# A two-layer hybrid mixer kernel: another order and other instructions in the attention loop

## Chip, core and metric

The kernel runs on one core of a Trainium2 chip. The metric is device time in microseconds (us), the median of three runs. The engines are named as in the profile: PE is TensorE (PEld its weight loads), DVE VectorE, ACT ScalarE, POOL GpSimd, SP the engine that issues most DMAs.

## What is computed

Two layers run over 1024 latent tokens and 256 context tokens of width 1024. Each layer normalises and modulates its input, multiplies it with one wide input matrix, feeds four mixers (attention, pooling, a state space, a gated MLP), gates their outputs and multiplies with an output matrix. The change touches the attention alone:

```python
q = (_rms(cq, g_q) @ w_uq).reshape(b, n, MLA_HEADS, MLA_NOPE + MLA_ROPE)      # 4 heads, 64 + 32
s = einsum('bqhd,bkhd->bhqk', qn, k_nope) + einsum('bqhr,bkr->bhqk', qr, k_rope)
p = softmax(s * 96 ** -0.5)                   # maximum over the keys taken off first
o = einsum('bhqk,bkhd->bqhd', p, v)           # then times the SiLU gate
```

Latent queries see 1280 keys, context queries (first layer only) the 256 context keys. All in float32.

## The kernel before, in words

Scores are kept transposed: keys on the partitions, queries on the columns. One step of the loop (`w`, line 1477) is one head `h` of a pair of heads `v` on 256 queries. Its 1280 keys make five PSUM banks of two key tiles each (`BANKS`, line 1212), each bank 128 x 512. Layer 1 has 8 pairs, 16 steps; layer 0 has the same and two short pairs for the context queries, with one bank a step.

The order on PE, DVE, ACT and POOL is written out by hand (line 1476): each engine runs its instructions as the Python calls come. One step does this:

- `scores(v, h, 1..4)`: 24 products of 256 columns fill banks 1 to 4 (three products for each key tile: high and low parts). ACT copies bank 0 into `acc` (line 1338), DVE takes the maximum of `acc` and each further bank, column halves apart (line 1340), and folds the two halves (line 1342).
- `vals(.., 0)`: probabilities times values of the pair before, in float32. `PVS` (line 37) says how many of the step's five key tiles go into each of three slots. The two heads write the two halves of the output's partitions.
- `maxima`: PE transposes `acc` (line 1354), DVE reduces over what are now columns (line 1356), negates and splits the result in a high and a low part (`m4`, lines 1358 and 1359).
- `vals(.., 1)`; then `rows`: PE turns `m4` into four rows (line 1365) and DVE spreads them into `row` (line 1367).
- `scores` of bank 0 of the next head (line 1502), into the sixth buffer of the ring of score banks (five `mm` and one `tp`).
- in even steps `finish`: sums of the probabilities of the pair before by a product with ones (line 1431), and their reciprocals over 128 x 256 (line 1435). In odd steps the two products with the gate (lines 1437 and 1438).
- `shift` (line 1369): for each bank a product of four rows with ones adds minus the maximum to the scores (line 1376); then ACT takes the exponentials (line 1389), which frees the bank, and POOL adds them up.

Transposed maxima, sums and one score bank in six share a pool of two PSUM banks (`tp`): a tile taken from it waits until the one before in its bank has been read. In every even step the query projection of the next pair stands between scores and values (`q_pair`), and in some odd steps that of the next 256 queries (`q_chunk`), with DVE's part of `q_pair` (line 1300) ahead of `rows`.

Of the kernel before, what the change touches and what calls it, by code (L numbers as in the profile page):

```python
# [12 lines left out]
F32 = mybir.dt.float32  # L13
# [23 lines left out]
PVS = (((0, 2), (2, 5), (5, 5)), ((0, 2), (2, 5), (5, 5)), ((0, 2), (2, 5), (5, 5)), ((0, 3), (3, 5), (5, 5)))  # L37
# [38 lines left out]
def tile_hybrid_backbone(ctx: ExitStack, tc: tile.TileContext, A):  # L76
# [23 lines left out]
    stg = [""]  # L100
# [64 lines left out]
    rmask = const.tile([4, 2], F32, name="rmask")  # L165
    add(V, rmask, ident[0:4, 0:2], ident[0:4, 2:4])
    ones4 = const.tile([4, 128], F32R, name="ones4")
    V.tensor_copy(ones4, ones[0:4, :].to_broadcast([4, 128]))
# [1045 lines left out]
    def attention(l, last, blocks, out):  # L1214
# [99 lines left out]
        def scores(v, h, banks):  # L1314
# [8 lines left out]
            for i, kts in list(enumerate(BANKS if c0 < NLAT else BANKS[0:1]))[banks.start:banks.stop]:  # L1323
# [11 lines left out]
                for x in range(2):  # L1335
                    a, p = acc[:, n * x:n * x + n], ps[:, n * x:n * x + n]
                    if i == 0:
                        d["first"] = lambda: S.copy(acc, d["b"][0])
                    else:
                        tt(V, a, a, p, ALU.max)  # L1340
# [8 lines left out]
        def maxima(v, h):  # L1349
            d = st[v, h]  # L1350
            stg[0] = "mx"
            d["tp"] = tp = tp_ps()
            for j in range(2):
                T.transpose(tp[:, 128 * j:128 * j + 128], d["acc"][:, 128 * j:128 * j + 128], ident)
            m = sml.tile([128, 2], F32, tag="mx", name="mx")
            V.tensor_reduce(out=m, in_=tp[:, 0:n].rearrange("p (j k) -> p j k", j=2), axis=AX.X, op=ALU.max)
            d["m4"] = m4 = sml.tile([128, 4], F32, tag="m4", name="m4")
            ts(V, m4[:, 0:2].bitcast(F32R), m, -1.0, ALU.mult)
            stt(m4[:, 2:4], m, -1.0, m4[:, 0:2], ALU.mult, ALU.subtract)

        def rows(v, h):

            d = st[v, h]
            tp = d["tp"][0:4, 256:384]
            T.transpose(tp, d["m4"], ident)
            d["row"] = row = sml.tile([4, 2, 128], F32R, tag="row", name="row", bufs=2)
            mul(V, row, tp.unsqueeze(1).to_broadcast([4, 2, 128]), rmask.unsqueeze(2).to_broadcast([4, 2, 128]))

        def shift(v, h):

            c0, pr = pairs[v]
            d = st[v, h]
            stg[0] = "sh"
            rv = d["row"].rearrange("p j q -> p (j q)").unsqueeze(1).to_broadcast([4, 2, n])
            for ps in d["b"]:
                T.matmul(ps, lhsT=ones4, rhs=rv, start=False, stop=True, skip_group_check=True)  # L1376
# [44 lines left out]
        def finish(v):  # L1421
# [8 lines left out]
            for h in range(2):  # L1430
                T.matmul(tp[64 * h:64 * h + 64, 0:n], lhsT=ones.to_broadcast([128, 64]), rhs=st[v, h]["sm"][:, 0:n],
                         start=True, stop=True, skip_group_check=True)
            yield "fdve"
            rs = qp[0].tile([128, n], F32, tag="rs", name="rs", bufs=2) if v < nv - 1 else s2("rs")[:, 0:n]
            V.reciprocal(out=rs, in_=tp[:, 0:n])
            yield "av"
            mul(V, gs, st[v][:, 0:n], gs)
            mul(V, gs, rs, gs)
# [37 lines left out]
        with tc.manual_schedule(engines={mybir.EngineType[x] for x in MAN}):  # L1476
            for w in range(2 * nv):
# [16 lines left out]
                k = [range(5 * h + i, 5 * h + j) for i, j in PVS[w % 4]]  # L1494
# [6 lines left out]
                if w + 1 < 2 * nv:  # L1501
                    scores((w + 1) // 2, 1 - h, range(0, 1))
                vals(v, w, k, 2)
                if h and short:
                    go("fend")
                    go("fdve")
                if h:
                    go("av")
                if not short:
                    go("fend")  # L1510
                    go("fdve")
# [7 lines left out]
                shift(v, h)  # L1519
                if w == 2 * fresh[-1] - 3:  # L1520
                    out.scales()
# [19 lines left out]
            go("fdve")  # L1541
# [509 lines left out]
```

## Time and profile before

| | |
|---|---|
| median of three runs | 1442.95 us (1437.25 to 1455.37) |
| profiled execution | 1443.26 us, span 1441.5 us |
| granted TensorE clock, mean | 0.94 |
| busy share | PE 88%, PEld 69%, DVE 65%, POOL 38%, ACT 32% |
| chain that ended last | PE 51%, DVE 28%, issue 7%, POOL 6%, DMA 3%, ACT 3% |
| attention loops | 481 to 672 us (layer 0), 1177 to 1343 us (layer 1) |

The span is divided by engine; an engine that is off the chain of waits may idle for nothing. The two loops hold 357 us of the 1441.5 us. Within them one step takes 9 to 10 us, and the question in each is which wait ends last before `shift` can run.

### The profile page before, as it was taken

To read this page: it belongs to the slowest core of one execution; us is meant where nothing else is said; L and a number is where in the kernel's file an instruction comes from. 1 tells how busy PE (TensorE), PEld (TensorE's weight loads), DVE (VectorE), ACT (ScalarE), POOL (GpSimd) and SP (SyncE) were. 2 spreads that over 40 slices of the span, in tenths; PEclk is the share of its full clock that TensorE was granted. 3 is DMA by queue.
4 is the path that set the end of the run, shared out by engine and by line. 5 is a ranking of instruction groups with operands and counts; after the bars stand their busy time and mean duration, and the time that the engine had idled before them with its cause. 6 is when DMAs were issued, how large, how long until landed. Compare 5 with 4: busy or idle time off the path is not lost.

```text
span 1441.5 us, 20269 instructions
## 1 busy us (share of the span) xinstructions
PE 1271.1 (88%) x7558; PEld 992.0 (69%) x7558; DVE 937.8 (65%) x1974; ACT 464.8 (32%) x879; POOL 552.8 (38%) x580
## 2 busy tenths in 40 slices
PE   4877986999999998999999769987699999999997
PEld 1555764779888766766777657765488787766785
DVE  8685399623552576757799882699426447767566
ACT  2341220120343644445233422301213454544300
POOL 2476241301002345655444591314001126656343
PEclk9988997999998999999999979998799999999999
DMA  9435321665321100014122454412752020000421
GB/s 314 143 103 179 122 86 46 152 178 132 89 53 33 27 22 1 1 45 131 45 82 95 107 155 147 122 44 59 149 146 65 8 59 23 15 16 16 146 103 73
DMA packets 124679, 127.33 MB, mean 88 GB/s; under 512 B 40908, under 2 KB 98724, under 8 KB 124582
## 3 DMA queue, kind: packets, MB, share of 16 engines
q1 hardware_dynamic: 118886, 111.86, 26.3%
q0 software_dynamic: 2880, 9.54, 2.8%
q10 hardware_dynamic: 2816, 4.65, 0.9%
q8 instruction: 59, 0.97, 0.3%
q14 instruction: 38, 0.31, 0.1%
HBM read 97.47 MB, written 25.94 MB: 86 GB/s over the span
## 4 chain that ended last, share of the span: by engine, by line
PE 51%; DVE 28%; issue 7%; POOL 6%; DMA 3%; ACT 3%; SPq 1%; POOLq 0%; ACTq 0%; DVEq 0%
PE mm_sc L1330 7%; PE mm_out L1632 6%; PE mm_in L154 5%; PE mm_in L152 5%; DVE H L131 5%; PE mm_in L153 5%; PE av L1411 3%; DVE stmp L131 3%; DVE z L148 3%; PE mm_sc L1376 2%; DVE op L131 2%; DVE acc L131 2%; POOL op L131 1%; DVE xres L145 1%; PE tp_sc L1330 1%
## 5 line engine op out<-in xcount | busy, mean ns | idle before, releaser
L154 PE MATMUL mm_in<-hT,wlo 128*128 128x512 f32 (+1 forms) x696 | 264.6, 381 | 26.9 <-DVE wlo L131 26.9
L152 PE MATMUL mm_in<-hT,whi 128*128 128x512 f32 (+1 forms) x696 | 270.4, 390 | 0.4 <-ACT whi L635 0.4
L153 PE MATMUL mm_in<-hT,whi 128*128 128x512 f32 (+1 forms) x696 | 264.8, 381 | 5.8 <-POOL hT L131 3.1
L154 PEld LDWEIGHTS mm_in<-hT,wlo 128*128 128x128 f32 x696 | 137.6, 198 | 53.3 <-DVE wlo L131 29.4
L152 PEld LDWEIGHTS mm_in<-hT,whi 128*128 128x128 f32 x696 | 137.8, 199 | 35.8 <-issue 14.2
L1632 PE MATMUL mm_out<-wo,yh 128*128 128x512 f32 x576 | 161.4, 394 | 0.5 <-POOL wo L131 0.4
L153 PEld LDWEIGHTS mm_in<-hT,whi 128*128 128x128 f32 x696 | 138.2, 199 | 31.1 <-POOL hT L131 5.7
L1632 PEld LDWEIGHTS mm_out<-wo,yh 128*128 128x128 f32 x576 | 107.5, 189 | 25.5 <-issue 1.0
L635 ACT CAST whi<-wraw 128x1024 fp32r<-128x1024 f32 x38 | 42.6, 1122 | 192.4 <-PE mm_in L153 142.8
L131 DVE TENSOR_TENSOR acc<-acc,mm_sc 128x256 f32<-128x256 f32 x216 | 77.4, 417 | 39.9 <-PE mm_sc L1330 36.8
L131 DVE TENSOR_TENSOR wlo<-wraw,whi 128x1024 fp32r<-128x1024 f32 x38 | 58.0, 1532 | 67.1 <-ACT whi L635 61.0
L131 POOL TENSOR_TENSOR psum<-pE 128x512 f32<-128x512 f32 (+1 forms) x36 | 47.1, 1308 | 135.8 <-ACT pE L1389 135.8
L1632 PE MATMUL mm_out<-wo,yl 128*128 128x512 f32 x288 | 92.0, 392 | 0.6 <-POOL yl L131 0.6
L131 POOL TENSOR_TENSOR psum<-psum,pL 128x512 f32<-128x512 f32 x64 | 83.1, 1298 | 5.0
L131 DVE TENSOR_TENSOR H<-H,stmp 128x80 f32<-128x80 f32 x248 | 75.2, 362 | 0.8
L131 DVE TENSOR_TENSOR stmp<-a,H 128x160 f32<-128x160 f32 x124 | 54.8, 476 | 14.5 <-POOL pws L131 7.2
L144 POOL TENSOR_SCALAR srs<-smv 128x1 f32<-128x1 f32 x18 | 5.6, 312 | 152.6 <-DVE smv L1062 152.6
L1389 ACT ACTIVATE pE<-mm_sc 128x512 f32<-128x512 f32 x55 | 30.6, 594 | 102.3 <-PE mm_sc L1376 102.3
L1632 PEld LDWEIGHTS mm_out<-wo,yl 128*128 128x128 f32 x288 | 54.3, 189 | 12.5 <-POOL yl L131 1.0
L144 POOL TENSOR_SCALAR rs_z<-mv_z 128x1 f32<-128x1 f32 x18 | 18.5, 1029 | 114.7 <-DVE mv_z L1664 114.7
L1783 ACT ACTIVATE G<-mm_in 128x512 f32<-128x512 f32 (+1 forms) x40 | 22.2, 554 | 115.9 <-PE mm_in L154 115.9
L1330 PE MATMUL mm_sc<-QA,KT 96*128 96x256 f32 x372 | 56.8, 305 | 0.0
(360 smaller groups left out, 2805.8 us busy)
## 6 DMA issues: line engine op xcount, KB each, us to landing
wmod<-in_w_mod_dram SPq DMA_DIRECT2D x48, 512.0 KB, 4.5
wraw<-in_w_in_dram SPq DMA_DIRECT2D x36, 512.0 KB, 4.4
wor<-in_w_out_dram SPq DMA_DIRECT2D x16, 512.0 KB, 3.6
s5u<-Sd SPq DMA_DIRECT2D x8, 640.0 KB, 7.1
xd<-z SPq DMA_DIRECT2D x10, 512.0 KB, 2.7
xin<-in_x_dram SPq DMA_DIRECT2D x8, 512.0 KB, 7.6
Ed<-E ACTq DMA_DIRECT2D x16, 256.0 KB, 3.2
Rd<-bldR POOLq DMA_DIRECT2D x16, 256.0 KB, 3.9
```

The costliest lines, as they stand in the source:

```text
L131: return e.tensor_tensor(out=out, in0=a, in1=b, op=op)
L144: return e.tensor_scalar(out=out, in0=a, scalar1=s1, scalar2=None, op0=op0)
L148: return V.scalar_tensor_tensor(out=out, in0=a, scalar=s, in1=b, op0=op0, op1=op1)
L152: T.matmul(out, lhsT=ahi, rhs=bhi, start=start, stop=False)
L153: T.matmul(out, lhsT=ahi, rhs=blo, start=False, stop=False)
L154: T.matmul(out, lhsT=alo, rhs=bhi, start=False, stop=stop)
L635: copy(hi, raw)
L1330: T.matmul(out, lhsT=K[:, e, 128 * kt_:128 * kt_ + 128], rhs=Q[:, f], start=(x == 0 and y == 0), stop=False, skip_group_check=True)
L1376: T.matmul(ps, lhsT=ones4, rhs=rv, start=False, stop=True, skip_group_check=True)
L1389: S.activation(out=p, in_=ps, func=AF.Exp, scale=QSCALE)
L1411: T.matmul(st[v][64 * h:64 * h + 64, 0:n], lhsT=Vt[:, BANKS[i // 2][i % 2], 64 * head:64 * head + 64], rhs=st[v, h]["pt"][i // 2][:, n * ( ...
L1632: T.matmul(a[1][nh], lhsT=y[u][:, k, :], rhs=self.W[k][:, v, 512 * nh:512 * nh + 512], start=(k == 0 and u == 0 and v == 0), stop=(k == KC ...
```

## The change

Line numbers with a prime are those of the changed kernel.

- **Shift.** `row` now fills all 128 partitions; bank `i` takes partitions 32(i mod 4) and the next one, as a product of two rows. Four banks so lie in four different 32-row tiles of the array, the fifth in the first again.
- **Rows.** The transposed maxima are no longer split on DVE. PE multiplies each of the two columns, spread over 128 columns, with the identity (line 1364', float32), which puts the maxima on every partition; DVE makes the high parts on one set of partitions and the low on the other with two instructions of 128 x 256 (lines 144' and 148').
- **Order.** Bank 0 of the next head's scores comes behind the shift products; two key tiles of values take its place ahead of them.
- **Maximum.** One DVE instruction of 512 columns a bank instead of two of 256.
- **Sums.** Sums become columns: four products with a column of ones (line 1438'), a reciprocal of 128 x 4, and in the odd step four products that spread them again (`sb`, line 1447'); DVE multiplies the gate straight from there.

```diff
-PVS = (((0, 2), (2, 5), (5, 5)), ((0, 2), (2, 5), (5, 5)), ((0, 2), (2, 5), (5, 5)), ((0, 3), (3, 5), (5, 5)))
+PVS = ((0, 2), (2, 3), (3, 5))
...
-                for x in range(2):
-                    a, p = acc[:, n * x:n * x + n], ps[:, n * x:n * x + n]
...
-                        tt(V, a, a, p, ALU.max)
+                    tt(V, acc, acc, ps, ALU.max)
...
-            ts(V, m4[:, 0:2].bitcast(F32R), m, -1.0, ALU.mult)
-            stt(m4[:, 2:4], m, -1.0, m4[:, 0:2], ALU.mult, ALU.subtract)
...
-            tp = d["tp"][0:4, 256:384]
-            T.transpose(tp, d["m4"], ident)
-            d["row"] = row = sml.tile([4, 2, 128], F32R, tag="row", name="row", bufs=2)
-            mul(V, row, tp.unsqueeze(1).to_broadcast([4, 2, 128]), rmask.unsqueeze(2).to_broadcast([4, 2, 128]))
+            tp = d["tp"][:, 256:512]
+            for j in range(2):
+                T.matmul(tp[:, 128 * j:128 * j + 128], lhsT=d["m"][:, j:j + 1].to_broadcast([128, 128]), rhs=ident,
+                         start=True, stop=True, skip_group_check=True)
+            d["row"] = row = sml.tile([128, n], F32R, tag="row", name="row", bufs=2)
+            ts(V, row, tp, par[:, 0:1], ALU.mult)
+            stt(row, tp, par[:, 1:2], row, ALU.mult, ALU.add)
...
-            for ps in d["b"]:
-                T.matmul(ps, lhsT=ones4, rhs=rv, start=False, stop=True, skip_group_check=True)
+            for i, ps in enumerate(d["b"]):
+                r = slice(32 * (i % 4), 32 * (i % 4) + 2)
+                T.matmul(ps, lhsT=ones4[r], rhs=d["row"][r].unsqueeze(1).to_broadcast([2, 2, n]), start=False, stop=True,
+                         skip_group_check=True)
...
-                T.matmul(tp[64 * h:64 * h + 64, 0:n], lhsT=ones.to_broadcast([128, 64]), rhs=st[v, h]["sm"][:, 0:n],
-                         start=True, stop=True, skip_group_check=True)
-            yield "fdve"
-            rs = qp[0].tile([128, n], F32, tag="rs", name="rs", bufs=2) if v < nv - 1 else s2("rs")[:, 0:n]
-            V.reciprocal(out=rs, in_=tp[:, 0:n])
+                for j in range(2):
+                    T.matmul(tp[:, 2 * h + j:2 * h + j + 1], lhsT=st[v, h]["sm"][:, 128 * j:128 * j + 128], rhs=ones,
+                             start=True, stop=True, skip_group_check=True)
+            rq = sml.tile([128, 4], F32, tag="rq", name="rq")
+            V.reciprocal(out=rq, in_=tp[:, 0:4])
+            yield "fbc"
+            stg[0] = "sb"
+            tp = tp_ps()
+            for h in range(2):
+                for j in range(2):
+                    T.matmul(tp[64 * h:64 * h + 64, 128 * j:128 * j + 128],
+                             lhsT=rq[:, 2 * h + j:2 * h + j + 1].to_broadcast([128, 64]), rhs=ident,
+                             start=True, stop=True, skip_group_check=True)
+            mul(V, gs, tp[:, 0:n], gs)
             yield "av"
             mul(V, gs, st[v][:, 0:n], gs)
-            mul(V, gs, rs, gs)
...
                 rows(v, h)
                 go("row")
-                if w + 1 < 2 * nv:
-                    scores((w + 1) // 2, 1 - h, range(0, 1))
                 vals(v, w, k, 2)
                 if h and short:
                     go("fend")
-                    go("fdve")
+                    go("fbc")
+                elif h:
+                    go("fbc")
                 if h:
                     go("av")
...
                 shift(v, h)
+                if w + 1 < 2 * nv:
+                    scores((w + 1) // 2, 1 - h, range(0, 1))
+                exps(v, h)
```

How the order on PE looks in an odd step of layer 1 (the step of 1205 to 1215 us), before. `av` are the values, `tp_mx` the transposed maxima, `mm_sc` and `tp_sc` score banks; what a row waits for stands in brackets, by engine:

```order
L1411 MATMUL av<-pL,Vt 64x256 x6
L1354 MATMUL tp_mx<-ident,acc 128x128 [waits DVE_49,PE_49]
L1354 MATMUL tp_mx<-ident,acc 128x128
L1411 MATMUL av<-pM,Vt 64x256 x4
L1365 MATMUL tp_mx<-ident,m_10250 4x128 [waits DVE_49]
L1330 MATMUL mm_sc<-QA,KT_9681 128x256 [waits Activation_49]
L1330 MATMUL mm_sc<-QA,KT_9681 128x256 x5
L1376 MATMUL mm_sc<-row,ones_91 128x512 [waits DVE_49]
L1376 MATMUL mm_sc<-row,ones_91 128x512
L1376 MATMUL tp_sc<-row,ones_91 128x512
```

The same place in the changed program:

```order
L1417 MATMUL av<-pL,Vt 64x256 x4
L1355 MATMUL tp_mx<-ident,acc 128x128 [waits DVE_49]
L1355 MATMUL tp_mx<-ident,acc 128x128
L1417 MATMUL av<-pL,Vt 64x256 x2
L1364 MATMUL tp_mx<-ident,mx 128x128 [waits DVE_49]
L1364 MATMUL tp_mx<-ident,mx 128x128
L1417 MATMUL av<-pM,Vt 64x256 x4
L1447 MATMUL tp_sb<-ident,rq 64x128 [waits DVE_49,PE_49]
L1447 MATMUL tp_sb<-ident,rq 64x128 x3
L1376 MATMUL mm_sc<-row,ones_93 128x512 x2
L1376 MATMUL tp_sc<-row,ones_93 128x512
```

The scores have gone from ahead of the shift, four value products stand there, and then `tp_sb`. `tp_sb` takes the bank that `tp_mx` held and waits for DVE's last read of it, which is the second instruction that makes `row`; the shift behind it has no wait of its own any more. In an even step the same holds for the sums:

```order
L1364 MATMUL tp_mx<-ident,mx 128x128 [waits DVE_49]
L1364 MATMUL tp_mx<-ident,mx 128x128
L1417 MATMUL av<-pE,Vt 64x256 x2
L1417 MATMUL av<-pL,Vt 64x256 x2
L1438 MATMUL tp_sm<-ones,psum 128x1 [waits DVE_49,PE_49,Pool_49]
L1438 MATMUL tp_sm<-ones,psum 128x1
L1438 MATMUL tp_sm<-ones,psum 128x1 [waits Pool_49]
L1438 MATMUL tp_sm<-ones,psum 128x1
L1376 MATMUL mm_sc<-row,ones_93 128x512
```

In the kernel before, the sums of the even step stood at the same place behind the same wait (line 1431). DVE in the odd step before, from the fold of the maxima to the products with the gate:

```order
L131 TENSOR_TENSOR acc<-acc 128x256
L1356 TENSOR_REDUCE mx<-tp_mx 128x2
L144 TENSOR_SCALAR m_10250<-mx 128x2
L148 SCALAR_TENSOR_TENSOR m_10250<-mx,m_10250 128x2
L131 TENSOR_TENSOR row<-tp_mx,rmask 4x256
L131 TENSOR_TENSOR G_0_7527<-av,G_0_7527 128x256
```

and in the changed program:

```order
L131 TENSOR_TENSOR acc<-acc 128x256
L1357 TENSOR_REDUCE mx<-tp_mx 128x2
L144 TENSOR_SCALAR row<-tp_mx,par 128x256
L148 SCALAR_TENSOR_TENSOR row<-tp_mx,par,row 128x256
L131 TENSOR_TENSOR G_0_7515<-tp_sb,G_0_7515 128x256
L131 TENSOR_TENSOR G_0_7515<-av,G_0_7515 128x256
```

The two small instructions between the reduction and PE's next product are gone; between that product and the shift stand two instructions of 256 columns where one stood.

## Rows read from the trace of the kernel before

**Rows 1.** Busy time by stretch, the two attention loops (us, busy and count, clock, DMA)

```profile
481.00:672.00 191.00, 176.16 (x1146) 127.59 (x1144) 128.66 (x286) 90.59 (x181) 107.80 (x95) 0.95 0.08 26
1177.00:1343.00 166.00, 156.19 (x1045) 114.60 (x1045) 112.12 (x256) 80.21 (x157) 100.97 (x86) 0.97 0.08 25
```

**Rows 2.** Timeline, PE in an odd step (start, length, engine, line, what, idle before)

```profile
1205.55 0.50 PE L1376 MATMUL mm_sc<-row,ones 4*128 4x512 f32 x1
...
1206.92 0.78 PEld L1330 LDWEIGHTS mm_sc<-QB,KT 128*128 128x128 f32 x6 [0.37 <-ACT pE L1389]
...
1209.97 1.52 PE L1411 MATMUL av<-pL,Vt 128*64 128x256 f32 x12
...
1212.01 0.41 PE L1354 MATMUL tp_mx<-ident,acc 128*128 128x128 f32 x2 [0.52 <-DVE acc L131]
...
1213.86 0.27 PE L1365 MATMUL tp_mx<-ident,m 128*4 128x128 f32 x1 [0.43 <-DVE m L148]
...
1213.89 0.95 PE L1330 MATMUL mm_sc<-QA,KT 96*128 96x256 f32 x6
...
1214.77 0.73 PE L1376 MATMUL mm_sc<-row,ones 4*128 4x512 f32 x2
```

**Rows 3.** Timeline, ACT and DVE in the same step

```profile
1206.15 0.60 ACT L1389 ACTIVATE pE<-mm_sc 128x512 f32<-128x512 f32 x1 [3.97 <-PE mm_sc L1376]
...
1210.87 0.99 DVE L131 TENSOR_TENSOR acc<-acc 128x256 f32<-128x256 f32 x1
...
1212.45 0.42 DVE L1356 TENSOR_REDUCE mx<-tp_mx 128x2 f32<-128x256 f32 x1 [0.59 <-PE tp_mx L1354]
...
1213.11 0.69 DVE L148 SCALAR_TENSOR_TENSOR m<-mx,m 128x2 f32<-128x2 f32 x1
...
1214.17 0.41 DVE L131 TENSOR_TENSOR row<-tp_mx,rmask 4x256 fp32r<-4x256 f32 x1 [0.36 <-PE tp_mx L1365]
```

**Rows 4.** Timeline, DVE and PE at the end of the next, even step

```profile
1221.42 0.42 DVE L1356 TENSOR_REDUCE mx<-tp_mx 128x2 f32<-128x256 f32 x1 [0.60 <-PE tp_mx L1354]
...
1223.14 0.42 DVE L131 TENSOR_TENSOR QB<-qp,QB 64x256 fp32r<-64x256 f32 x1
...
1223.59 0.41 DVE L131 TENSOR_TENSOR row<-tp_mx,rmask 4x256 fp32r<-4x256 f32 x1
...
1224.15 0.65 PE L1431 MATMUL tp_sm<-psum,ones 128*64 128x256 f32 x4 [0.34 <-DVE row L131]
...
1224.73 0.96 PE L1376 MATMUL mm_sc<-row,ones 4*128 4x512 f32 x3
...
1224.84 1.76 DVE L1435 RECIPROCAL rs<-tp_sm 128x256 f32<-128x256 f32 x1 [0.84 <-PE tp_sm L1431]
```

**Rows 5.** Timeline, end of the odd step after it, which has a query projection

```profile
1232.35 0.42 DVE L1356 TENSOR_REDUCE mx<-tp_mx 128x2 f32<-128x256 f32 x1 [1.54 <-PE tp_mx L1354]
...
1233.69 0.27 PE L1365 MATMUL tp_mx<-ident,m 128*4 128x128 f32 x1
...
1234.59 1.21 PE L1376 MATMUL mm_sc<-row,ones 4*128 4x512 f32 x4
```

**Rows 6.** Timeline, PE elsewhere: products shaped like the added ones

```profile
414.91 0.71 PE L1095 MATMUL tp_rms<-ident,rrs 128*128 128x128 f32 x4 [0.45 <-POOL rrs L131]
...
416.05 0.95 PE L1084 MATMUL tp_rms<-ones,sq 128*128 128x1 f32 x8
...
418.38 1.13 PE L1095 MATMUL tp_rms<-ident,rrs 128*128 128x128 f32 x8
...
346.51 1.09 PE L1041 MATMUL tp_sgu<-sgw,vnt 128*64 128x128 f32 x16
```

**Rows 7.** Groups by line and shape, DVE (busy us, mean ns; idle before)

```profile
L131 DVE TENSOR_TENSOR z<-mm_out,gl 128x512 f32<-128x512 f32 x30 | 20.4, 681 | 33.9 <-PE mm_out L1632 33.8
L145 DVE TENSOR_SCALAR vnt<-mm_sgv,smv,srs 128x256 f32<-128x256 f32 x18 | 9.8, 543 | 14.0 <-POOL srs L131 14.0
L148 DVE SCALAR_TENSOR_TENSOR tp_sgu<-tp_sgu,cols,sgw 128x256 f32<-128x256 f32 x18 | 8.5, 484 | 2.1 <-PE tp_sgu L1041 1.9
```

More of the change, by code (lines that the diff above doesn't have):

```diff
@@ L164, in tile_hybrid_backbone @@
     D.dma_start(edge, A["edge"])
[L165 to L168, printed above, removed]
+    par = const.tile([128, 2], F32, name="par")
+    V.tensor_reduce(out=par[:, 1:2], in_=ident.rearrange("p (c r) -> p r c", r=2)[:, 1:2, :], axis=AX.X, op=ALU.add)
+    ts(V, par[:, 0:1], par[:, 1:2], 2.0, ALU.mult, -1.0, ALU.add)
+    ts(V, par[:, 1:2], par[:, 1:2], -1.0, ALU.mult)
+    ones4 = const.tile([128, 128], F32R, name="ones4")
+    V.tensor_copy(ones4, ones.to_broadcast([128, 128]))
     cv = s2("cv")[0:16, 0:128]
@@ L1334, in scores @@
                     continue
-                for x in range(2):
-                    a, p = acc[:, n * x:n * x + n], ps[:, n * x:n * x + n]
-                    if i == 0:
-                        d["first"] = lambda: S.copy(acc, d["b"][0])
-                    else:
-                        tt(V, a, a, p, ALU.max)
+                if i == 0:
+                    d["first"] = lambda: S.copy(acc, d["b"][0])
+                else:
+                    tt(V, acc, acc, ps, ALU.max)
                 if i == 4:
@@ L1354, in maxima, with exps @@
                 T.transpose(tp[:, 128 * j:128 * j + 128], d["acc"][:, 128 * j:128 * j + 128], ident)
-            m = sml.tile([128, 2], F32, tag="mx", name="mx")
+            d["m"] = m = sml.tile([128, 2], F32, tag="mx", name="mx")
             V.tensor_reduce(out=m, in_=tp[:, 0:n].rearrange("p (j k) -> p j k", j=2), axis=AX.X, op=ALU.max)
-            d["m4"] = m4 = sml.tile([128, 4], F32, tag="m4", name="m4")
-            ts(V, m4[:, 0:2].bitcast(F32R), m, -1.0, ALU.mult)
-            stt(m4[:, 2:4], m, -1.0, m4[:, 0:2], ALU.mult, ALU.subtract)
         def rows(v, h):
             d = st[v, h]
-            tp = d["tp"][0:4, 256:384]
-            T.transpose(tp, d["m4"], ident)
-            d["row"] = row = sml.tile([4, 2, 128], F32R, tag="row", name="row", bufs=2)
-            mul(V, row, tp.unsqueeze(1).to_broadcast([4, 2, 128]), rmask.unsqueeze(2).to_broadcast([4, 2, 128]))
-        def shift(v, h):
+            tp = d["tp"][:, 256:512]
[5 more added lines that the diff above has]
+            stt(row, tp, par[:, 1:2], row, ALU.mult, ALU.add)
+        def shift(v, h):
+            d = st[v, h]
+            stg[0] = "sh"
+            for i, ps in enumerate(d["b"]):
+                r = slice(32 * (i % 4), 32 * (i % 4) + 2)
+                T.matmul(ps, lhsT=ones4[r], rhs=d["row"][r].unsqueeze(1).to_broadcast([2, 2, n]), start=False, stop=True,
+                         skip_group_check=True)
+        def exps(v, h):
             c0, pr = pairs[v]
             d = st[v, h]
-            stg[0] = "sh"
-            rv = d["row"].rearrange("p j q -> p (j q)").unsqueeze(1).to_broadcast([4, 2, n])
-            for ps in d["b"]:
-                T.matmul(ps, lhsT=ones4, rhs=rv, start=False, stop=True, skip_group_check=True)
             e, l1, l2 = wh("pE", F32), None, None
@@ L1493, in attention @@
                 go("act mm")
-                k = [range(5 * h + i, 5 * h + j) for i, j in PVS[w % 4]]
+                k = [range(5 * h + i, 5 * h + j) for i, j in PVS]
                 vals(v, w, k, 0)
@@ L1510, in attention @@
                     go("fend")
-                    go("fdve")
                 go("dve")
@@ L1540, in attention @@
             go("fend")
-            go("fdve")
+            go("fbc")
             go("av")
```

## The prediction

> **What bounds the kernel now.** The change touches the two attention loops only, so I read the busy time of those stretches first [rows 1]: 191 and 166 us, 357 of 1441.5, with PE busy for 92% and 94% of them and a granted clock of 0.95 and 0.97. PE looks like the bound, so the next view is the timeline of single steps, to see whether PE waits and for whom. Take the odd step whose shift starts at 1205.55 [rows 2]. PE idles three times: 0.37 us for ACT's first exponential, 0.52 us for DVE's folded maximum, 0.43 us for DVE's `m`. The next shift starts at 1214.77, so the step takes 9.22 us.
>
> What the reader is to see is one loop of dependence: shift, exponential that frees a bank, scores, maxima on DVE, transposes, reduction, `m`, transposed back, `row`, next shift. PE's values are laid into its gaps. Two stretches of it matter.
>
> From shift to scores: the shift starts at 1205.55, ACT's first exponential 0.60 us later [rows 3], and the bank that it frees lets the next scores go at 1206.92, which is 1.37 us after the shift began. Five shift products fill just that time; if they were shorter, the scores would still wait for the exponential.
>
> From reduction to shift: call the end of the reduction R. In the odd step R = 1212.45 + 0.42 = 1212.87 [rows 3] and the shift comes at R + 1.90. In an even step R = 1221.84 and the shift comes at 1224.73 = R + 2.89 [rows 4]: `QA` and `QB` stand ahead of `row` on DVE, and the sums wait for `row` (0.34 us idle), then hold PE until the shift. In an odd step with a query projection R = 1232.77 and the shift comes at R + 1.82 [rows 5].
>
> **Part by part.** The sum is made against the profiled execution, 1443.26 us, 0.3 us above the median of 1442.95.
>
> *Row-tiled shift and bank 0 behind it.* No row shows two 32-row tiles at work together. Lower bound for the five products: two rounds, four together and then one, which is what two in a row take now, 0.73 us less the part that lies under the next product, so some 0.6 us [rows 2]. Upper bound: 1.37 us as now. I take 0.6 us, since tiles of another kind do overlap here: 12 value records, which go to the two halves of the output's partitions in turn, take 1.52 us, 0.13 us each, while a single product takes 0.50 [rows 2]. Then bank 0 of the next head (0.88 us, from 1213.89 to 1214.77 [rows 2]) runs from 0.6 to about 1.4 us after the shift began, and bank 1 starts when the exponential frees it, at 1.37 us as before. So the whole stretch from shift to R keeps its length: price 0. What is gained is only that bank 0 no longer stands ahead of the shift; whether that pays is decided by what stands there now. The Trainium skill, "TensorE: Matmul & The Clock Gate", section "Measured speedup vs the span model", gives 3.07 times for four row tiles of 512 columns, by which the five products would take about 0.6 us and my sum would stay; without any overlap it would be the first rival's.
>
> *Between reduction and shift, odd step.* Removed: `m` and its split, with 0.69 us for the slower [rows 3], the transpose of 0.27, `row` of 0.41. Added, in series: 0.06 us to PE (1213.80 to 1213.86 [rows 2, 3]); four records of product with the identity, 0.71 us [rows 6], a group of the very same form; 0.03; two DVE instructions of 128 x 256. For these, the nearest rows are 0.41 (`row`) and 0.42 (the reduction, 256 columns from PSUM) below [rows 3], 0.54 and 0.48 above [rows 7]. I take 0.43 and 0.45, nearer to the former, because each reads the same 256 columns from PSUM, with 0.03 between. Then 0.15 us to PE (1224.00 to 1224.15 [rows 4]): R + 1.86. Now `sb`, because the program makes it wait for the second of these instructions and the shift stands behind it. It is eight records of 128 columns into 64 partitions: half of the 16 in 1.09 us, 0.55, if the two halves overlap; 1.13 if they don't [rows 6]. Four records for one half come before the four for the other, so they overlap in part: 0.75, and the next product starts 0.07 before its end, as the shift does behind the sums [rows 4]. Shift at R + 2.54 against R + 1.90: 0.64 us longer (0.38 to 1.16). With a query projection, against R + 1.82, 0.72 longer. The two value tiles ahead of `sb` are hidden: eight records against four in [rows 6] say that four more cost PE 0.42 us, so the values begin at about R + 0.48, take 8 x 0.13, and end at R + 1.52. There are 14 such steps (8 and 8 pairs, less the first of each layer), half of them with a projection: 14 x 0.68 = 9.5 us (5.9 to 16.8).
>
> *Even step.* `QA` and `QB` now follow R directly, 0.04 + 2 x 0.42 us [rows 4], which hides the product with the identity (done at R + 0.77). The two instructions of `row` then end at R + 1.82, the sums start at R + 1.97. They are eight records with one column, 0.95 us [rows 6], same form, less 0.07: shift at R + 2.85 against R + 2.89. That is 0.04 shorter (0.10 shorter to 0.10 longer), in 10 steps. In four steps the sums take another bank and don't wait for `row`; they follow the values and end at about R + 2.4, 0.5 shorter. Together -2.4 us (-3.0 to -1.0). The two first even steps have no sums: the shift follows `row` at R + 1.97 instead of R + 2.31, -0.7 together.
>
> *The rest.* The reciprocal falls from 1.76 us to about that of a tiny instruction; in the loop it ran beside shift and scores [rows 4], so this is worth nothing there. At the end of each loop it is exposed, but sums and `sb` are longer: -0.5 us together. In the two short steps sums, reciprocal and `sb` stand in one row ahead of the shift: +2 us together. A maximum of 512 columns takes 0.68 [rows 7] where two of 256 take 0.75; only the last of a step counts, and only where the fold is waited for: -0.5 (0 to -1.6). The constants at the start cost under 1 us of DVE, beside loads.
>
> Sum: 9.5 - 2.4 - 0.7 - 0.5 + 2 - 0.5 = +7 us, 1450 us. With all bounds low (5.9 - 3.0 - 0.7 - 0.5 + 1 - 1.6) it is 1444, all high (16.8 - 1.0 + 2) it is 1461.
>
> PE's own stream gives no other answer: in a pair of steps the shift saves 1.5 us, while two products with the identity, longer sums and `sb` add 0.8, 0.3 and 0.7. Where a step is bound by PE, it gains nothing either.
>
> **Rivals.**
>
> *The row tiles run one after the other* (the change doesn't do what it says). For: nothing in the trace shows row tiles overlapping, and the products stream four-byte numbers. Against: the overlap of the two partition halves. Then bank 0 would be done at 1.37 + 0.8 after the shift's start instead of at 1.4, and every further bank comes 0.8 us later, in 32 steps: +26 us, 1476, slower. It decides from the point where the five products take over 0.6 us.
>
> *The clock falls.* More of PE's waiting is now in one piece: in the odd step the values of 8 records end at about 1211.0, 1.0 us before the transposes, and 0.35 us are idle ahead of `sb`. The loops already spend about (1 - 0.95) x 2 x 191 = 19 us and 10 us at 1.2 GHz [rows 1]. If that doubles, 29 us more run at half speed and lose half speed and lose about half of it: +15, 1465. Against: the idle time replaces waits of 0.52 and 0.43 us.
>
> *The chain gets shorter.* If `sb`, sums and the DVE pair take their lower bounds, and the fold, 0.99 us in this step [rows 3] and shorter where POOL does less beside it, gains 0.3 us in each of 32 steps: 1444 - 10 = 1434. For: the slow 0.69 us of `m` shows that small DVE work is held up and leaves the chain. Against: the POOL additions start at the same distance from the shift.
>
> **Numbers.** Forecast 0.61, serial tiles 0.12, clock 0.13, shorter chain 0.14. The likeliest case gives 1450 us, own range 1442 to 1461. The range from 1430 to 1472 leaves out the serial tiles and the tails, under 2 in 10. A measurement tells 2%, 29 us, from no change: under 1414 or over 1472. Slower is most of the serial tiles and the far end of the clock, 0.13; faster needs nearly 1 us in each of 32 steps, more than R + 1.86 leaves at any price: 0.04; same 0.83.
>
> **What would show it.** Shift products of one step that start within 0.1 us of each other (if 0.23 apart, the first rival). Scores of bank 1 still waiting for ACT at 1.3 to 1.4 us after the shift. `sb` waiting for DVE, and the shift right behind it, at about R + 2.5 in odd steps and R + 2.8 in even ones. A granted clock in the loops well under 0.95 would be the second rival. I am wrong if R itself moves against the shift by more than 0.3 us, or if `sb` does not wait.

## The result and the profile after

The changed kernel takes 1469.64 us (median of 4 runs, 1466.62 to 1471.60) against 1445.66 us for the kernel before in the same comparison: a ratio of 1.0157 (95% interval 1.0122 to 1.0193), 24 us slower. That lies inside the range of 1430 to 1472 and within 2%, as forecast, but 20 us above the forecast of 1450 and outside the likeliest case's own range (1442 to 1461): a change of +7 us was forecast, +24 was measured. The profiled execution takes 1466.62 us, its span is 1464.8 us, and its mean granted clock 0.937 (before 0.940).

Busy time by stretch, the two loops, answering to [rows 1] (PE, PEld, DVE, ACT, POOL, clock, DMA):

```profile
485.00:684.00 199.00, 183.28 (x1305) 136.14 (x1304) 108.83 (x202) 91.09 (x179) 106.45 (x93) 0.96 0.08 26
1189.00:1366.00 177.00, 166.66 (x1194) 125.06 (x1192) 100.25 (x177) 81.79 (x156) 98.72 (x83) 0.95 0.07 23
```

The loops are longer by 8 and 11 us. DVE works 32 us less in them, PE 18 us more. The time at half speed, (1 - clock) x 2 x length, was 29 us in [rows 1] and is 34 us here; taken from the first shift of each loop to its last, it was 24 and is 34. The clock is a small part; what it cost is worked out further down.

An odd step, PE's timeline, answering to [rows 2]:

```profile
1220.73 0.49 PE L1376 MATMUL mm_sc<-row,ones 2*128 2x512 f32 x1
1220.74 0.49 PE L1376 MATMUL tp_sc<-row,ones 2*128 2x512 f32 x1
1220.74 0.72 PE L1376 MATMUL mm_sc<-row,ones 2*128 2x512 f32 x3
1221.39 1.68 PE L1333 MATMUL mm_sc<-QB,KT 128*128 128x256 f32 x12
...
1226.85 0.44 PE L1355 MATMUL tp_mx<-ident,acc 128*128 128x128 f32 x2 [0.61 <-DVE acc L131]
...
1229.70 0.66 PE L1447 MATMUL tp_sb<-ident,rq 128*64 128x128 f32 x8 [0.17 <-DVE row L148]
1230.30 0.50 PE L1376 MATMUL mm_sc<-row,ones 2*128 2x512 f32 x2
```

The row tiles do work together: the first four products start within 0.01 us (the third line above holds three, of which the last starts at 1221.07, in the first tile again), and the next scores follow 0.66 us after the first of them, where five products in a row filled 1.37 us. From the 3.07 times for four row tiles that the Trainium skill gives in "TensorE: Matmul & The Clock Gate", section "Measured speedup vs the span model", the estimate was about 0.6 us; the trace is near it with 0.66. The scores of bank 1 follow those of bank 0 without a gap, 1.36 us after the shift; forecast was 1.37.

ACT and DVE in the same step, answering to [rows 3]:

```profile
1221.33 0.60 ACT L1395 ACTIVATE pE<-mm_sc 128x512 f32<-128x512 f32 x1 [4.08 <-PE mm_sc L1376]
...
1223.18 0.69 DVE L131 TENSOR_TENSOR acc<-acc,mm_sc 128x512 f32<-128x512 f32 x1 [1.85 <-PE mm_sc L1333]
...
1227.32 0.42 DVE L1357 TENSOR_REDUCE mx<-tp_mx 128x2 f32<-128x256 f32 x1 [0.53 <-PE tp_mx L1355]
1228.55 0.48 DVE L144 TENSOR_SCALAR row<-tp_mx,par 128x256 fp32r<-128x256 f32 x1 [0.80 <-PE tp_mx L1364]
1229.07 0.48 DVE L148 SCALAR_TENSOR_TENSOR row<-tp_mx,par,row 128x256 fp32r<-128x256 f32 x1
```

R, the end of the reduction, is 1227.74. `row` ends at R + 1.81, `sb` waits for it (0.17 us idle), and the shift comes at R + 2.56; forecast was R + 2.54. The end of the next, even step, answering to [rows 4]:

```profile
1236.99 0.42 DVE L1357 TENSOR_REDUCE mx<-tp_mx 128x2 f32<-128x256 f32 x1 [0.64 <-PE tp_mx L1355]
1237.56 0.79 POOL L131 TENSOR_TENSOR psum<-psum 128x256 f32<-128x256 f32 x1
1237.79 0.84 DVE L131 TENSOR_TENSOR QB<-qp,QB 64x256 fp32r<-64x256 f32 x1
...
1239.18 0.48 DVE L148 SCALAR_TENSOR_TENSOR row<-tp_mx,par,row 128x256 fp32r<-128x256 f32 x1
1239.81 1.02 PE L1438 MATMUL tp_sm<-ones,psum 128*128 128x1 f32 x8 [0.61 <-DVE row L148]
1240.76 0.51 PE L1376 MATMUL mm_sc<-row,ones 2*128 2x512 f32 x3
1240.87 0.18 DVE L1441 RECIPROCAL rq<-tp_sm 128x4 f32<-128x4 f32 x1 [1.21 <-PE tp_sm L1438]
```

Here the shift comes at R + 3.35, not at R + 2.85. `QB` takes 0.84 us instead of the 0.42 of [rows 4], because it started inside a POOL instruction and ended only 0.28 us behind it; the row then ends late, the sums wait 0.61 us for it, and the shift stands behind them.

I took R and the shift's start from the timelines of every step. R to shift, summed over both loops, grew from 81.1 to 100.5 us: 14 odd steps by 11.4 us, 14 even ones by 4.8, the first two steps of each layer by 2.1, the four short ones by 1.1. Shift to R grew by 1.5 us only. Ahead of the loops' first shift the trace is 3.8 us longer, 0.7 of it in that first step.

### The profile page after: what moved, and what is told of

It reads as the page before. It is cut to its first block, busy times and chain, and to the rows that moved or that the text cites. A ratio compares the mean times of both kernels' runs of the same rounds, so it can differ in the third digit from the quotient of the medians.

```text
span 1464.8 us, 20658 instructions
## 1 busy us (share of the span) xinstructions
PE 1292.6 (88%) x7882; PEld 1017.2 (69%) x7882; DVE 904.0 (62%) x1812; ACT 467.2 (32%) x879; POOL 549.7 (38%) x580
## 3 DMA queue, kind: packets, MB, share of 16 engines
q8 instruction: 62, 1.02, 0.3%
## 4 chain that ended last, share of the span: by engine, by line
PE 52%; DVE 28%; POOL 7%; issue 6%; ACT 3%; DMA 3%; SPq 1%; DVEq 0%; POOLq 0%; ACTq 0%
PE mm_out L1648 7%; PE mm_sc L1333 7%; PE mm_in L152 5%; PE mm_in L154 5%; PE mm_in L153 5%; DVE H L131 5%; DVE stmp L131 3%; PE av L1417 3%; DVE z L148 3%; DVE acc L131 2%; DVE op L131 2%; PE tp_mx L1364 1%; PE tp_sc L1333 1%; PE mm_sc L1376 1%; POOL op L131 1%
## 5 line engine op out<-in xcount | busy, mean ns | idle before, releaser
L131 DVE TENSOR_TENSOR acc<-acc,mm_sc 128x512 f32<-128x512 f32 x108 | 74.3, 688 | 72.9 <-PE mm_sc L1333 59.5
L131 DVE TENSOR_TENSOR H<-H,stmp 128x80 f32<-128x80 f32 x248 | 71.4, 342 | 0.8
```

Of the source, the lines that this page charges most:

```text
L131: return e.tensor_tensor(out=out, in0=a, in1=b, op=op)
```

## The experiments

My theory was that the loss stands in series between R and the shift: `sb` in odd steps, longer sums behind a later row in even ones. Rivals were the new order or the row tiles themselves, and the clock. The table has all runs; "odd" and "even" are the mean R to shift of 14 steps each, the sums run over both loops of the profiled execution. Ratios are to the kernel before, timed beside each run.

| kernel | us | ratio (95%) | odd | even | sum R to shift | sum shift to R |
|---|---|---|---|---|---|---|
| before | 1446 | 1 | 1.77 | 2.64 | 81.1 | 251.0 |
| changed | 1469.6 | 1.0157 (1.0122 to 1.0193) | 2.59 | 2.98 | 100.5 | 252.6 |
| changed, old sums | 1451.3 | 1.0042 (1.0011 to 1.0073) | 1.87 | 2.63 | 82.9 | 251.0 |
| changed, one row tile | 1500.1 | 1.0404 (1.0359 to 1.0448) | 2.55 | 2.97 | 101.8 | 285.6 |
| changed, old order and split | 1495.8 | 1.0359 (1.0309 to 1.0409) | 3.13 | 3.75 | 120.5 | 257.0 |
| changed, old split | 1493.8 | 1.0332 (1.0304 to 1.0360) | 3.17 | 3.41 | 116.0 | 258.0 |
| changed, `sb` early | 1466.8 | 1.0151 (1.0102 to 1.0199) | 1.87 | 3.06 | 91.3 | 258.0 |
| changed, `QA`, `QB` behind the row | 1469.7 (one run) | - | 2.58 | 2.91 | 98.3 | 253.0 |
| before, new sums | 1478.9 | 1.0255 (1.0215 to 1.0295) | 2.31 | 3.04 | 97.2 | 262.1 |
| before, broadcast rows | 1481.9 | 1.0256 (1.0207 to 1.0305) | 2.45 | 3.44 | 104.3 | 257.0 |
| before, sums and `QA`, `QB` moved | 1445.6 | 1.0021 (0.9990 to 1.0052) | 1.73 | 1.93 | 70.2 | 263.6 |
| changed with old sums, moved alike | 1461.2 | 1.0099 (1.0068 to 1.0130) | 1.87 | 2.04 | 72.3 | 265.7 |
| before, moved, one product later | 1434.1 | 0.9929 (0.9900 to 0.9957) | 1.73 | 1.88 | 69.2 | 255.0 |
| changed with old sums, same | 1450.2 | 1.0040 (1.0014 to 1.0067) | 1.87 | 1.87 | 70.2 | 257.9 |

**The old sums in the changed kernel.**

```diff
-                    T.matmul(tp[:, 2 * h + j:2 * h + j + 1], lhsT=st[v, h]["sm"][:, 128 * j:128 * j + 128], rhs=ones,
...
-            V.reciprocal(out=rq, in_=tp[:, 0:4])
-            yield "fbc"
...
+                T.matmul(tp[64 * h:64 * h + 64, 0:n], lhsT=ones.to_broadcast([128, 64]), rhs=st[v, h]["sm"][:, 0:n],
...
+            yield "fdve"
...
+            V.reciprocal(out=rs, in_=tp[:, 0:n])
```

> The changed kernel with the old sums and reciprocal (two 64-column products, 128x256 reciprocal, no sb). Theory 1 (the loss is the work that now stands in series between R, the end of the maximum's reduction, and the first shift product): odd steps fall from R+2.56 to about R+1.9, even steps from a mean of R+2.98 to R+2.6 to 2.8, together 14 x 0.66 + 14 x 0.25 = about 13 us less than the changed kernel: 1457 us (1452 to 1462), about 1.008 of the kernel before. Rival 2 (the order or the row tiles themselves cost, the sums do not): 1465 us or more. Rival 3 (lower granted clock): steps outside the stretch R to shift carry the loss, and the time stays above 1463.

It gave 1451.3 us, 18 us less than the changed kernel (17 by the ratios) and just outside the expected 1452 to 1462, with odd steps at 1.87 and the sum of shift to R within 2 us. The sums are the larger part of the loss; all the rest together costs 6 us (0.42%).

**One row tile.**

```diff
-                r = slice(32 * (i % 4), 32 * (i % 4) + 2)
+                r = slice(0, 2)
```

> The changed kernel with all five shift products on rows 0 and 1, so that they run one after the other. Theory 1: the next head's bank-0 scores start 1.3 to 1.4 us after the first shift product instead of 0.66, and since bank 1 follows them, each of 34 steps grows by about 0.65 us: 1469 + 22 = 1491 us (1480 to 1495). Rival (the first exponential gates all scores, so the row tiles carry nothing): 1469 us, within 5.

```profile
1290.26 1.42 PE L1376 MATMUL mm_sc<-row,ones 2*128 2x512 f32 x5
1291.61 0.97 PE L1333 MATMUL tp_sc<-QB,KT 128*128 128x256 f32 x6
...
1293.39 3.06 DVE L131 TENSOR_TENSOR acc<-acc,mm_sc 128x512 f32<-128x512 f32 x4 [2.53 <-PE mm_sc L1333]
```

PE's and DVE's timeline of a step: scores start 1.35 us after the shift, and the first maximum at 3.13 us instead of 2.45 (1223.18 against 1220.73 above). It costs 30 us over the changed kernel, more than the 22 expected, with 33 us in shift to R. The 19 steps that ran at full clock in both kernels grew by 0.6 us each, 11.5 us together, as expected; the other 22 us lie in 15 steps that ran in part at half speed (granted clock 0.89 in the first loop), and why the clock fell there, no run shows. The rival, that the exponential gates all scores, is out: it gates bank 1, bank 0 waits for the shift products alone.

**The old order, with and without the old split of the values.**

```diff
-PVS = ((0, 2), (2, 3), (3, 5))
+PVS = (((0, 2), (2, 5), (5, 5)), ((0, 2), (2, 5), (5, 5)), ((0, 2), (2, 5), (5, 5)), ((0, 3), (3, 5), (5, 5)))
...
                 go("row")
+                if w + 1 < 2 * nv:
+                    scores((w + 1) // 2, 1 - h, range(0, 1))
...
                 shift(v, h)
-                if w + 1 < 2 * nv:
-                    scores((w + 1) // 2, 1 - h, range(0, 1))
```

> The changed kernel with the next head's bank-0 scores ahead of the shift products again, and the old split of the value products. Theory 1: bank-0 scores fit into the 1.0 us in which the row is made and bank 1 waits for the first exponential in both orders, so no change: 1469 us (1464 to 1474). Rival 2 (the new order costs, because the scores that filled the wait for the row now stand behind it): 15 to 24 us less, 1445 to 1454.

Neither expectation held: 1495.8 us, 26 more. The edit had changed two things, so a second run put back the split alone (the `PVS` lines above):

> The changed kernel with the old split of the value products alone (three keys instead of one between the transposes and the broadcast, none behind it); next head's scores stay behind the shift products. If the run with the old order lost its 27 us by the late broadcast: row 0.4 us later, odd R+2.97, even about R+3.75, 14 x 0.4 + 14 x 0.75 = 16 us, 1469 + 16 = 1485 us (1478 to 1495). If it lost them by the place of the scores: 1469, within 4.

It gave 1493.8 us, as the first branch says; the two intervals overlap, so with the old split the place of bank 0 shows no cost, and the split does. PE's and DVE's timeline of an odd step of that run, R = 1289.10:

```profile
1288.57 1.08 PE L1417 MATMUL av<-pM,Vt 128*64 128x256 f32 x8
1289.59 0.71 PE L1364 MATMUL tp_mx<-ident,mx 128*128 128x128 f32 x4
1291.49 0.66 PE L1447 MATMUL tp_sb<-ident,rq 128*64 128x128 f32 x8 [1.19 <-DVE row L148]
...
1290.34 0.48 DVE L144 TENSOR_SCALAR row<-tp_mx,par 128x256 fp32r<-128x256 f32 x1 [1.23 <-PE tp_mx L1364]
```

The broadcast stands behind eight value records, starts at R + 0.49 instead of R + 0.06, and PE then idles 1.19 us with nothing left to put there.

**The new sums alone, and the broadcast rows alone, in the kernel before.**

Each is the change's own piece of code put into the kernel before: sums, reciprocal, `sb` and their places in the loop in the one (its core below), `m`, the broadcast and the two operations on `row` in the other, with `par` and with shift products on rows 0 and 1.

```diff
                 if h and short:
                     go("fend")
-                    go("fdve")
+                    go("fbc")
+                elif h:
+                    go("fbc")
...
                 if not short:
                     go("fend")
-                    go("fdve")
```

```diff
-            T.transpose(tp, d["m4"], ident)
+            for j in range(2):
+                T.matmul(tp[:, 128 * j:128 * j + 128], lhsT=d["m"][:, j:j + 1].to_broadcast([128, 128]), rhs=ident,
...
+            ts(V, row, tp, par[:, 0:1], ALU.mult)
+            stt(row, tp, par[:, 1:2], row, ALU.mult, ALU.add)
```

> The kernel before with the column sums, the 128x4 reciprocal and the broadcast product sb alone. Theory 1: odd steps R+1.9 to about R+2.65 (14 x 0.75 = 10.5 us), even steps 0.44 us longer (four products of 0.25 instead of 0.58 us; 14 x 0.44 = 6 us): 1446 + 17 = 1463 us (1456 to 1466), 1.011 of the kernel before. Rival 2 (order and row tiles cost): 1446 to 1450.

> The kernel before with the broadcast rows alone (order, split of the values, shift products one after the other, old sums). From the run with the old order: with eight value products ahead of the broadcast the row's first operation starts at R+1.23 in odd and R+1.67 in even steps and takes 1.0 us with its second: odd R+2.3 (before 1.77), even about R+3.3 (before 2.64), 14 x 0.5 + 14 x 0.65 = 16 us: 1446 + 16 = 1462 us (1455 to 1468). Rival (my prediction's view: the rows' chain is no longer than the old one): 1446, within 4.

Both cost 35 to 37 us (by the medians beside them and by the ratios), twice what was expected. R to shift grew by 16 us with the sums, as expected, and by 23 with the rows (odd 2.45, even 3.44), where 16 were. The rest is in shift to R (11 and 6 us) and outside the loops. The loops of the new sums alone ran more at half speed, by stretch:

```profile
494.83:685.73 190.90, 177.78 (x1181) 133.87 (x1180) 105.68 (x268) 84.15 (x169) 105.30 (x92) 0.92 0.07 22
1204.30:1368.48 164.18, 157.91 (x1038) 121.20 (x1037) 91.45 (x236) 71.53 (x141) 91.46 (x79) 0.91 0.05 15
```

By the measure used above that is 60 us at half speed, from first shift to last, against 24 in the kernel before. Why the clock fell there, no run shows, so what the sums cost by themselves in the old order isn't settled by this run; the 16 us in R to shift are. In this kernel `sb` doesn't wait: bank 0 covers the row, and `sb` holds PE for its own time.

**`sb` moved ahead of the transposes, `QA` and `QB` behind the row.** Two single moves in the changed kernel. For the first, `sb` writes to the free columns of the values' bank, so that it needs no bank of its own:

```diff
                 vals(v, w, k, 0)
+                if h and not short:
+                    go("fbc")
                 maxima(v, h)
...
             stg[0] = "sb"
-            tp = tp_ps()
+            tp = st[v][:, n:2 * n]
```

> The changed kernel with the product sb put ahead of the odd step's transposes, where TensorE waits 0.6 to 0.7 us for acc, into the free columns of the values' bank; nothing else. Theory (the price of the sums is their place between R and the shift): odd steps fall from R+2.56 to about R+1.9, the stretch from shift to R grows by 0.1 at most, so 14 x 0.55 = 8 us less than the changed kernel's 1469: 1461 us (1457 to 1465). Rival (0.6 us of TensorE work costs the same wherever it stands): 1469, within 3.

PE's timeline of an odd step of this run (R = 1276.43):

```profile
1274.70 0.65 PE L1447 MATMUL av<-ident,rq 128*64 128x128 f32 x7
1275.57 0.41 PE L1355 MATMUL tp_mx<-ident,acc 128*128 128x128 f32 x2 [0.22 <-DVE acc L131]
...
1278.30 0.49 PE L1376 MATMUL tp_sc<-row,ones 2*128 2x512 f32 x1
```

In the trace the move does what was expected: PE's wait for `acc` shrinks from 0.61 to 0.22 us, odd steps stand at R + 1.87, and such a step at full clock takes 8.95 us instead of 9.6. The time doesn't follow: 1466.8 us, an interval that holds both branches. Of the 9 us that R to shift lost, shift to R took 5 back, in steps that ran partly at half speed, and the unchanged stretch between the loops was 6 us longer than the changed kernel's (522.3 against 516.4). This run doesn't settle whether 8 us were gained.

For the second:

```diff
                 maxima(v, h)
-                go("m4")
                 vals(v, w, k, 1)
                 rows(v, h)
+                go("m4")
```

> The changed kernel with QA and QB put behind the row on VectorE, nothing else. If the even steps at R+3.35 come from QB (0.84 us beside POOL's fold) ahead of the row, they fall to R+2.9, set then by TensorE's own work (broadcast 0.71, values 1.08, sums 1.02); about 5 steps x 0.4 = 2 us, too little for the total: 1467 us (1460 to 1474). If the sums' wait sets them whatever VectorE does, they stay at 3.35.

PE and DVE at the end of an even step, R = 1284.05:

```profile
1286.01 1.02 PE L1438 MATMUL tp_sm<-ones,psum 128*128 128x1 f32 x8 [0.17 <-DVE row L148]
1286.96 0.49 PE L1376 MATMUL mm_sc<-row,ones 2*128 2x512 f32 x1
...
1285.38 0.48 DVE L148 SCALAR_TENSOR_TENSOR row<-tp_mx,par,row 128x256 fp32r<-128x256 f32 x1
1286.21 0.42 DVE L131 TENSOR_TENSOR QB<-qp,QB 64x256 fp32r<-64x256 f32 x1
```

The row ends at R + 1.81, the steps at 3.35 are gone, and 2.90 to 2.92 is left, or 2.70 where the sums don't wait (one step, whose sums took 1.84 us at half speed, came to 3.73). So `QB` was the cause of 3.35, in four steps, worth 1.8 us, which one run can't resolve in the total.

**A version that clears R to shift, in both kernels.** The old sums go ahead of the *odd* step's transposes, where PE waits, and `QA`, `QB` behind the row.

```diff
                 vals(v, w, k, 0)
+                if h:
+                    go("fend")
                 maxima(v, h)
-                go("m4")
                 vals(v, w, k, 1)
                 rows(v, h)
+                go("m4")
...
             stg[0] = "sm"
-            tp = tp_ps()
+            tp = st[v][:, n:2 * n]
```

> The kernel before with two moves: the two sum products go ahead of the next odd step's transposes (into the free columns of the values' bank, the reciprocal behind that step's row), and the next pair's two subtractions (QA, QB) go behind the row on VectorE. If the stretch R to shift is what counts: even steps fall from a mean of R+2.64 to R+1.9 to 2.0 (14 x 0.7 = 10 us), the reciprocal and two products of 2.6 us behind the odd row delay the first maximum by 0.2 (by 1.2 in the three steps with qf), 4 to 6 us back: 1446 - 5 = 1441 us (1434 to 1447). Rival (the work of TensorE alone counts): 1446.

> The changed kernel with the old sums, moved in the same two ways. Even steps fall from 2.63 (changed kernel with the old sums in their old place, 1451 us) to R+1.9 (14 x 0.7 = 10 us), 4 to 6 back at the first maximum: 1451 - 5 = 1446 us (1439 to 1452), odd steps R+1.87. Rival (the work of TensorE alone counts): 1451.

In the kernel before it came out level, in the changed one 0.6% above its own version with the old sums; both miss. R to shift fell to 1.84 to 1.87 nearly everywhere, 11 us in sum, and shift to R rose by 13 and 15 us. DVE's and POOL's timeline shows the new bound (kernel before, moved; shift at 1220.10; `acc<-acc` is the fold):

```profile
1219.84 1.74 DVE L1435 RECIPROCAL rs<-av 128x256 f32<-128x256 f32 x1
1221.50 0.35 DVE L131 TENSOR_TENSOR G<-av,G 128x256 f32<-128x256 f32 x1
1221.89 1.54 DVE L131 TENSOR_TENSOR G<-rs,G 128x256 f32<-128x256 f32 x1
1223.35 1.40 DVE L131 TENSOR_TENSOR acc<-acc,mm_sc 128x256 f32<-128x256 f32 x4
...
1226.02 1.26 POOL L131 TENSOR_TENSOR psum<-psum,pM 128x512 f32<-128x512 f32 x1
1226.11 1.46 DVE L131 TENSOR_TENSOR acc<-acc 128x256 f32<-128x256 f32 x1
```

The product G x rs takes 1.54 us beside POOL's first sum, where it took 0.42 to 0.50 in 17 of 18 places of the kernel before, and the first maximum starts 3.25 us after the shift instead of 2.5. That is 0.8 us, and such even steps grew by 1.4 (from 7.1 to 8.5 us). The rest is the fold: it now comes too late to end with POOL's third sum, starts inside the fourth and ends 0.29 us behind it, after 1.46 us. So the last runs put off that product (and let G x av go ahead of the reciprocal):

```diff
             yield "fdve"
+            mul(V, gs, st[v][:, 0:n], gs)
...
             V.reciprocal(out=rs, in_=tp[:, 0:n])
-            yield "av"
-            mul(V, gs, st[v][:, 0:n], gs)
+            yield "post"
             mul(V, gs, rs, gs)
...
                 go("m4")
+                if not h:
+                    go("post")
```

> The kernel before with the sums ahead of the odd step's transposes and QA, QB behind the row, as in the run that came out level (R to shift 1.84, but VectorE 3.5 us busy behind the odd row, so that the first maximum started 0.8 us late and shift to R in even steps rose from 7.1 to 8.47), and now with the last of that work, the product G x rs (1.30 us beside POOL), put off to the next even step behind its row; reciprocal and G x av (2.2 us) stay. If the VectorE queue behind the odd row took back the gain: shift to R in even steps falls to 7.1 to 7.3, about 11 steps x 1.2 = 13 us, 1446 - 12 = 1434 us (1428 to 1442), faster than both kernels. Rival (TensorE's work is the bound, wherever it stands): 1445.

> The same put-off product in the changed kernel with old sums moved: shift to R in even steps from 8.47 to about 7.1, R to shift 1.87: 1461 - 12 = 1449 us (1442 to 1455). Rival (TensorE's work is the bound): 1460.

Both came out within 1.2 us of the expectation, at 1434.1 and 1450.2 us; in the former five of the even steps went from 8.5 back to 7.1 us at full clock. DVE's timeline of the former, shift at 1252.34 and 1261.31:

```profile
1252.08 0.40 DVE L131 TENSOR_TENSOR G<-av,G 128x256 f32<-128x256 f32 x1
1252.41 1.74 DVE L1436 RECIPROCAL rs<-av 128x256 f32<-128x256 f32 x1
1254.80 0.75 DVE L131 TENSOR_TENSOR acc<-acc,tp_sc 128x256 f32<-128x256 f32 x2 [0.65 <-PE tp_sc L1330]
...
1261.89 0.43 DVE L131 TENSOR_TENSOR G<-rs,G 128x256 f32<-128x256 f32 x1
```

and a pair of its steps by stretch:

```profile
1243.36:1261.31 17.95, 17.57 (x126) 12.90 (x126) 13.97 (x33) 9.62 (x20) 13.21 (x12) 1.00 0.17 59
```

DVE is idle again before the first maximum, the put-off product takes 0.43 us, and PE is busy for 17.57 of 17.95 us. At 0.9929 (0.9900 to 0.9957) this version beats both kernels, with none of the change's edits in it.

## Why the prediction was right, and where it was wrong

The sum gave +7 us, and the two profiled executions differ by 23; its own upper bound was 1461 us. Of the 16 us between, 7 lie in the even steps, 3 in the first steps, 3 ahead of the loops and 2 in the odd steps. That 1469.6 still lies in the range is owed to the margin up to 2%; the clock, the rival priced nearest to it (1465), had little part in the loss. So much is luck.

- **Shift to R keeps its length, price 0**: right in sum (251.0 to 252.6 us), in part by luck. As forecast, the tiles take 0.66 us, bank 0 behind them starts at once, and the first exponential still comes 0.60 us after the shift; the run with one tile shows that without this a step at full clock takes 0.6 us more. Of the 21 steps that ran at full clock in both kernels, eight of nine long even ones keep their length within 0.1 us. But six odd ones went from 7.31 to 7.35 us down to 7.01 to 7.09, and the reason is a member that the loop of dependence lacked. The fold ends 0.26 to 0.31 us behind one of POOL's sums in 28 of 30 steps before and in 26 after, so it is POOL that sets R there. An odd step, before (shift at 1205.55, fold in [rows 3]) and after (shift at 1220.73):

```profile
1207.31 1.54 POOL L131 TENSOR_TENSOR psum<-pE 128x512 f32<-128x512 f32 x1 [3.73 <-ACT pE L1389]
1207.34 0.36 DVE L131 TENSOR_TENSOR qr<-qf,qr 128x256 fp32r<-128x256 f32 x1
1208.93 2.65 POOL L131 TENSOR_TENSOR psum<-psum,pL 128x512 f32<-128x512 f32 x2
...
1222.49 1.30 POOL L131 TENSOR_TENSOR psum<-pE 128x512 f32<-128x512 f32 x1 [5.34 <-ACT pE L1395]
1223.87 2.64 POOL L131 TENSOR_TENSOR psum<-psum,pL 128x512 f32<-128x512 f32 x2
1226.28 0.52 DVE L131 TENSOR_TENSOR acc<-acc 128x256 f32<-128x256 f32 x1
```

  Before, `qr`, a DVE operation for the next queries, stood behind the reciprocal of 1.76 us and ran beside POOL's first sum, which took 1.54 us; the next two sums end at 1211.58 and the fold at 1211.86. After, the reciprocal takes 0.18 us, `qr` is done before that sum, which takes 1.30 us, and the fold ends 6.07 us behind the shift instead of 6.31. With the old sums in the changed kernel five of these six steps are back at 7.32 us or more. So the reciprocal, priced at nothing in the loop, was worth some 0.25 us in such a step. All 21 steps together are 1.5 us shorter; the 13 that ran in part at half speed in one kernel or the other are 3.1 us longer.
- **Odd steps, +9.5 us**: right. R + 2.56 was measured for R + 2.54; it came to 11.4, 1.3 of it because before's mean was 1.77, not 1.86, and 0.5 because one step came at R + 3.01. Two misses cancel: the DVE pair took 0.48 + 0.48 instead of 0.43 + 0.45, and `sb` 0.60 us until the shift instead of 0.68.
- **Even steps, -2.4 us**: the step that failed, by sign. It measured +4.8. Half of the 7.2 us comes from the reading of before: I set all even steps at the R + 2.89 of [rows 4], and only seven of 14 stood at 2.81 to 2.89, the others at 2.35 to 2.43. One of those, DVE in the kernel before, R = 1262.38 and shift at 1264.81:

```profile
1262.63 0.16 DVE L148 SCALAR_TENSOR_TENSOR m<-mx,m 128x2 f32<-128x2 f32 x1
...
1263.61 0.41 DVE L131 TENSOR_TENSOR row<-tp_mx,rmask 4x256 fp32r<-4x256 f32 x1
```

  The split of `m` takes 0.16 us there, as in the other six of these, and 0.61 to 0.70 in the seven late steps, in each of which it starts inside a POOL instruction (0.69 in the odd step of [rows 3]). The other half comes from after: I put ten steps at 2.85 and four at 2.4, and there were six at 2.92, four at 3.35 (`QB` beside POOL) and four at 2.70, where the sums don't wait but PE's own stream of broadcast, values and sums (0.71, 1.08 and 1.02 us) takes that long.
- **First steps, -0.7 us for the even ones**: wrong; R to shift rose from 2.08 (I had 2.31) to 2.78 in each, as other value products of PE hold the broadcast back until R + 1.08 in the first of them, and the first odd steps, which I left out, rose by 0.7 us together. **Short steps, +2**: 1.1. **512-wide maximum, -0.5**: 0.69 us each, as priced, but they start 0.79 us apart and the last ends 5.51 us behind the shift, not 5.28: later, not earlier. It cost nothing, because the fold ends with POOL.
- **Serial tiles** (rival): out, by the tiles' starts. **Clock** (rival): 10 us more at half speed between first shift and last, worth the 3.1 us above. **Shorter chain** (rival): the fold did fall, from 0.99 to 0.52 us, but its end followed POOL's, which gave 0.25 us in six steps instead of 0.3 in 32.
- **Outside the loops**: I had priced nothing. The 3.1 us ahead of the first step lie in stretches that the change doesn't touch, but for some constants; in the 12 other traces the first shift of the loops comes between 489.6 and 498.2 us (before 489.24, changed 493.05), with old and new constants alike. I put it down to the spread between executions, which isn't shown more closely.

In all, R to shift +19.4 and shift to R +1.5, less 1.4 that lies in the first steps ahead of the two loops' first shift, make the loops 19.5 us longer; with 3.8 ahead, -0.3 between and 0.3 behind it is the 23.3 us between the two profiled executions. The sums are worth 17 to 18 of these by their own run, nearly all of it in R to shift (100.5 against 82.9 us); the rows cost 35 to 37 us alone in the old order, and tiles and split pay for most of that: without the one the changed kernel takes 30 us more, without the other 24. How the three share it isn't shown.

## What to carry to other kernels

Set up the loop of dependence and ask of each added instruction whether it stands between the last wait and the release; there every 0.1 us counts, and a product of PE that is "also just 0.6 us" is paid in full. A row of one step is not the row of all: tabulate the chain over every step before pricing, above all where a second engine decides between two durations. When work is moved out of the chain, price the queue that it lands in with the work that runs beside it there. And look whose end the last member of a loop really follows: here the fold ended with POOL's sum, whether DVE's maxima came 0.2 us earlier or later.

## What the runs showed of the hardware

In the attention loops a DVE instruction with all operands in SBUF and a POOL instruction exclude each other. Of 90 such DVE instructions that start inside a POOL instruction in the loops of the kernel before, 82 end only after it. In the moved kernel POOL's first sum and the product G x rs:

```profile
1221.86 1.29 POOL L131 TENSOR_TENSOR psum<-pE 128x512 f32<-128x512 f32 x1 [1.36 <-ACT pE L1389]
```

POOL's ends at 1223.15, the product, begun at 1221.89, at 1223.43. In the same way `QB` took 0.84 instead of 0.42 us and `m` 0.69 instead of 0.16, while maxima with one operand in PSUM kept their 0.69 to 0.75 us. It goes the other way too: seven of the other eight are `qr`, which begins 0.03 to 0.06 us behind POOL's first sum and runs its 0.36 us through, and that sum takes 1.54 to 1.58 us instead of 1.30. The Trainium skill, "SBUF — State Buffer", section "SBUF: two separate sides", says that the two engines share a port pair that one instruction holds for its whole length; these rows agree. Putting off one such product was worth 0.9% in one kernel and 0.6% in the other (1.0021 to 0.9929, 1.0099 to 1.0040).
